# Values and gates of the recurrence as one 2x2x2 block product in seven multiplications

## The chip, the core and the metric

The kernel runs on one core of a Trainium2 chip. The core has a matrix engine (TensorE, PE in the profile, with its weight loads as PEld), a vector engine (VectorE, DVE), an activation engine (ScalarE, ACT), a general engine (GpSimd, POOL), a queue that issues transfers (SyncE, SP) and 16 DMA engines. Every engine works through its own list of instructions in order and waits on semaphores for the others. The metric is the device time of one execution in microseconds; less is better.

## The reference, cut to what matters

```python
hn = rmsnorm(h, norm_mix_g[l])                 # 512 tokens x 1024
proj = hn @ w_in[l]
fq, fk, fv, ff, gq, gf, gi, gg = jnp.split(proj, split_idx, axis=-1)
...
rec = hgrn2_chunkwise(gq, gf, gi, lbs[l])      # gi: the values, 512 columns
rec = rmsnorm(rec, hgrn_norm_g[l]) * jax.nn.silu(gg...)   # gg: the gates, 512 columns
```

One layer follows: forgetting attention (fq, fk, fv, ff), the gated recurrence (gq, gf, gi, gg), an output projection, cross attention on 256 memory tokens, and an MLP with 4096 hidden columns. The change is in how gi and gg are computed: together they are the product of hn (512 x 1024) with 1024 columns of w_in.

## The kernel before

**Products.** Activations and weights are split into a high part (one conversion on ACT) and a low part (the difference, on DVE), and every product is three matmuls: high by high, high by low, low by high. Weights come as panels of 1 MB in two halves (a and b) of 512 KB. SP loads a half into one of two raw buffers (`wrN` in the profile, N the panel's number), ACT writes the high part `whN`, DVE the low part `wlN`; high and low parts have four buffers each, so two panels. A raw buffer can be loaded again when both parts are written, and a high or low buffer can be written again when PE is through with the half that lay there.

**Order.** PE's instructions run as the code writes them; ACT, DVE, POOL and SP have orders that a scheduler lays down when the kernel is built. `next_panel` (L216) loads up to two panels ahead of use. The panels are: 0 and 1 the forget logits gf, 2 and 3 the queries gq, 4 the first 256 value columns and the 8 forget columns of the attention (`proj_if`), 5 and 6 the gates (`proj_wide`), 7 and 8 the other 256 value columns together with 256 columns of fv (`proj_iv`), then 9 onwards the pairs of attention heads.

**Fill.** The recurrence needs an attention matrix inside each chunk, made in seven levels (m = 1, 2, 4 .. 64; L800 on PE, L806, L825 and L826 on DVE and POOL). Between two levels PE has nothing of its own to do, so `Fill` runs pieces of the projections there: `fill.run(us)` by a budget, `fill.until(name)` until a named projection is done. After the levels come the transposes `pa` of the attention matrix, the transposes `pk` of the keys, and the recurrence's steps (`po`, `pst`), which need the values `iv` and the gates `gg`.

**Block products in seven.** The MLP already multiplies 2 x 2 blocks in seven products (`SEVEN`), with sums of weight blocks made in DRAM: SP copies a block into a DRAM buffer (`copies`, so many behind each load by the table `COPIES`), and POOL adds another block to it with an accumulating transfer (`presum`, paced by PE's work through `PACE`).

**The residual.** `x_park` (L507) copies the transposed x of each column block out of PSUM and POOL writes it to DRAM (`xTd`), where the output projection fetches it later.

Of the kernel before, what the change touches and what calls it, by code (L numbers as in the profile page):

```python
# [16 lines left out]
P = 128  # L17
S = 512
# [20 lines left out]
NEG = -3.0e38  # L39
SEVEN = (1, 2, 3, 4, 5, 6, 7)  # L40
RAWS, HB, LOADS = 5, 4, 8
COPIES = {7: 2, 16: 1, 17: 0, 21: 1}
PACE = (183.0, 4.7), (306.0, 11.5)


@with_exitstack
def emit(
# [81 lines left out]
    def f(a):  # L129
        return a.bitcast(F32)  # L130
# [277 lines left out]
    gp.affine_select(out=tri[:, 0, :], in_=tri[:, 0, :], compare_op=ALU.is_ge, fill=0.0, base=0, pattern=[[1, P]], channel_multiplier=-1)  # L408


    hn_hi, hn_lo = act_tile("hn_hi"), act_tile("hn_lo")
    xTd = drp.tile([4, P, 2, S], F32, name="xTd")

# [73 lines left out]
    park = {}  # L487

    ms0 = sm(NT, "ms0")
    gv = cp.tile([P, 33], F32, name="gv")  # L490
# [14 lines left out]
        ve.scalar_tensor_tensor(hn_lo[:, c, :], xps[c], g_mix[:, c : c + 1], f(hn_hi[:, c, :]), op0=ALU.mult, op1=ALU.subtract)  # L505

    def x_park(c):  # L507
        part, new_ = c // 2, c // 2 not in park
        if new_:
            park[part] = s4([2, S], f"xT{part}")  # L510
        dst = park[part][:, c % 2, :]
        if c % 2 == 0:
            ac.activation(dst, xps[c], AF.Copy)
        else:
            ve.tensor_copy(dst, xps[c])
        if not new_:
            gp.dma_start(xTd[part], park[part])

    def x_sq(tb):
        junk = s4([D], f"x0j{tb}")  # L520
# [8 lines left out]
    with tc.manual_schedule(engines={mybir.EngineType.Activation, mybir.EngineType.DVE}):  # L529
# [121 lines left out]
    g_x, g_mem, g_ff, g_h = gv[:, 0:8], gv[:, 8:16], gv[:, 16:24], gv[:, 24:25]  # L651
    gate(3)
    forget(3)
    for hp in range(2):
        wt = next_panel()
        for j in range(2):
# [17 lines left out]
    def proj_wide(dsts, func, name):  # L674

        pss = [mm(f"{name}{tb}") for tb in range(NT - 1)] + [pvt(f"{name}3")]
        n = S // len(dsts)

        def done(tb, ps):
            for i, dst in enumerate(dsts):  # L680
                ac.activation(dst(tb), ps[:, i * n : (i + 1) * n], func, scale=r0[:, tb : tb + 1])

        yield from gemm_wide(pss, hn_hi, hn_lo, done)
# [4 lines left out]
    z = sm(32, "z")  # L688
    z3 = z.rearrange("p (t h) -> p t h", h=FH)

    def proj_if():
        wt = next_panel()
        for tb in range(NT):
            ps = mm(f"gi0{tb}", (WT + FH,))
            yield from gemm_tm(ps, wt, hn_hi, hn_lo, tb)
            ac.activation(iv[tb // 2][:, tb % 2, 0:WT], ps[:, 0:WT], AF.Identity, scale=r0[:, tb : tb + 1])
# [7 lines left out]
    fill.add(proj_if(), "ff")  # L704
    fill.add(new(gg, "gg"))
    fill.add(proj_wide([lambda tb: gg[tb // 2][:, tb % 2, :]], AF.Silu, "gg"), "gg")
# [6 lines left out]
    def proj_iv():  # L713
        yield from proj_wide([lambda tb: iv[tb // 2][:, tb % 2, WT:S], new_fv()], AF.Identity, "gi")

    fill.add(proj_iv(), "iv")

# [181 lines left out]
    load_mem(0)  # L899


    mx_hi, mx_lo = act_tile("mx_hi"), act_tile("mx_lo")
    St = None
    pending = None

# [1013 lines left out]
```

## Time and profile before

| | |
|---|---|
| median of 3 runs | 752.15 us (751.25 to 752.2) |
| the profiled execution | 751.99 us |
| its span, first to last instruction | 750.3 us |
| PE busy | 742.9 us of the span |
| DVE, ACT, POOL busy | 546.5, 444.7, 202.1 us |
| granted TensorE clock | 0.998 |

The profiled execution is 1.69 us longer than its span; that is what lies around the instructions. The first 62 us of the span are the norm, the forget logits and the queries, the levels run to 111 us, the recurrence to 158 us, then attention, output projection, cross attention and from 429 us the MLP.

### The profile page before, as it was taken

How to read it: one execution, taken by the hardware profiler on the slowest of the kernel's cores; microseconds unless marked ns; L12 is line 12 of the kernel's file. 1: busy time of each engine (PE TensorE's matmuls, PEld its weight loads, DVE VectorE, ACT ScalarE, POOL GpSimd, SP SyncE). 2: the span in 40 equal slices, each digit the busy share in tenths (PEclk: the TensorE clock that was granted, in tenths of full speed). 3: DMA queues.
4: the chain of work that ended last, by engine and by line, in shares of the span. 5: the costliest groups of instructions: out<-in, count | busy, mean ns of one | idle time of the engine just before them, and what ended most of it. 6: DMA issues, size and time to landing. Idle time of an engine off the chain costs nothing.

```text
span 750.3 us, 12293 instructions
## 1 busy us (share of the span) xinstructions
PE 742.9 (99%) x4581; PEld 649.6 (87%) x4581; DVE 546.5 (73%) x869; ACT 444.7 (59%) x749; POOL 202.1 (27%) x280
## 2 busy tenths in 40 slices
PE   9999999999999999999999999999999999999996
PEld 6889888888888888888888899898989899999985
DVE  5647873667878856645556898978787887878796
ACT  5655555556666742344434589666566757574864
POOL 7207531233433237621111212111111111100034
PEclk9999999999999999999999999999999999999999
DMA  8641987578957889985579799898989898978452
GB/s 250 200 116 58 298 262 228 172 231 269 289 187 224 265 225 210 193 165 122 121 165 197 114 250 238 237 226 247 230 218 235 220 247 214 240 198 232 133 113 113
DMA packets 109678, 152.92 MB, mean 204 GB/s; under 512 B 6145, under 2 KB 76074, under 8 KB 109618
## 3 DMA queue, kind: packets, MB, share of 16 engines
q1 hardware_dynamic: 85458, 112.52, 46.3%
q0 software_dynamic: 24000, 39.35, 30.1%
q8 instruction: 36, 0.59, 0.3%
q14 instruction: 24, 0.20, 0.1%
q10 hardware_dynamic: 160, 0.27, 0.1%
HBM read 147.91 MB, written 51.40 MB: 266 GB/s over the span
## 4 chain that ended last, share of the span: by engine, by line
PE 96%; DVE 1%; issue 1%; ACT 0%; POOL 0%; POOLq 0%; DVEq 0%
PE uU L1494 4%; PE uU L1496 4%; PE uU L1495 4%; PE U L1652 3%; PE U L1653 3%; PE U L1654 3%; PE uY L1495 2%; PE uY L1494 2%; PE uY L1496 2%; PE xk L1008 2%; PE xq L253 2%; PE wo L253 2%; PE xq L254 2%; PE xq L255 2%; PE xw L255 2%; PE xw L254 2%
## 5 line engine op out<-in xcount | busy, mean ns | idle before, releaser
L183 DVE TENSOR_TENSOR wlu<-wru,whu 128x1024 fp32r<-128x1024 f32 x53 | 64.2, 1225 | 28.0 <-ACT whu L179 27.9
L179 ACT ACTIVATE whu<-wru 128x1024 fp32r<-128x1024 f32 x53 | 55.9, 1058 | 43.7 <-PE U L1654 16.8
L183 DVE TENSOR_TENSOR wld<-wrd,whd 128x1024 fp32r<-128x1024 f32 x56 | 68.3, 1222 | 13.5 <-ACT whd L179 13.2
L179 ACT ACTIVATE whd<-wrd 128x1024 fp32r<-128x1024 f32 x56 | 59.0, 1053 | 12.6 <-PE uU L1495 5.2
L1652 PE MATMUL U<-whd,hb 128*128 128x512 f32 x120 | 46.8, 390 | 0.0
L1653 PE MATMUL U<-wld,hb 128*128 128x512 f32 x120 | 46.8, 390 | 0.0
L1654 PE MATMUL U<-whd,hb 128*128 128x512 f32 x120 | 46.7, 389 | 0.0
L1029 POOL TENSOR_SCALAR bi<-nF,Ft 128x128 f32<-128x128 f32 (+3 forms) x32 | 20.6, 652 | 59.8 <-PE pt L1065 38.8
L1494 PE MATMUL uU<-xs_hi,whu 128*128 128x256 f32 x128 | 36.3, 284 | 0.0
L1496 PE MATMUL uU<-xs_hi,wlu 128*128 128x256 f32 x128 | 36.2, 283 | 0.0
L1495 PE MATMUL uY<-xs_lo,whu 128*128 128x256 f32 x128 | 36.2, 283 | 0.0
L1494 PE MATMUL uY<-xs_hi,whu 128*128 128x256 f32 x128 | 36.2, 283 | 0.0
L1496 PE MATMUL uU<-x_hi,wlu 128*128 128x256 f32 x128 | 36.2, 283 | 0.0
L1496 PE MATMUL uY<-xs_hi,wlu 128*128 128x256 f32 x128 | 36.2, 283 | 0.0
L1495 PE MATMUL uU<-xs_lo,whu 128*128 128x256 f32 x128 | 36.2, 283 | 0.0
L1495 PE MATMUL uU<-x_lo,whu 128*128 128x256 f32 x128 | 36.2, 283 | 0.0
L1494 PE MATMUL uU<-x_hi,whu 128*128 128x256 f32 x128 | 36.2, 283 | 0.0
L444 POOL DMA_DIRECT2D wsd<-in_w_dram x16 | 17.9, 1116 | 63.6 <-PE xw L255 12.8
L1390 POOL DMA_DIRECT2D wrd<-in_w_dram x8 | 9.8, 1221 | 86.2 <-DVE wld L183 85.0
L444 POOL DMA_DIRECT2D wsu<-in_w_dram x14 | 17.1, 1218 | 48.9 <-PE xw L255 15.6
L1654 PEld LDWEIGHTS U<-whd,hb 128*128 128x128 f32 x120 | 22.5, 188 | 4.7
L1652 PEld LDWEIGHTS U<-whd,hb 128*128 128x128 f32 x120 | 22.6, 188 | 4.5
(944 smaller groups left out, 2605.2 us busy)
## 6 DMA issues: line engine op xcount, KB each, us to landing
wru<-in_w_dram SPq DMA_DIRECT2D x25, 512.0 KB, 7.9
wsd<-in_w_dram SPq DMA_DIRECT2D x24, 512.0 KB, 7.3
wrd<-in_w_dram SPq DMA_DIRECT2D x24, 512.0 KB, 4.3
wrd<-wsd SPq DMA_DIRECT2D x24, 512.0 KB, 4.9
wsu<-in_w_dram SPq DMA_DIRECT2D x21, 512.0 KB, 5.6
wru<-wsu SPq DMA_DIRECT2D x21, 512.0 KB, 6.1
wsd<-in_w_dram POOLq DMA_DIRECT2D x16, 512.0 KB, 7.8
wsu<-in_w_dram POOLq DMA_DIRECT2D x14, 512.0 KB, 6.9
```

Of the source, the lines that this page charges most:

```text
L179: at = ac.activation(hi, raw, AF.Copy)
L183: at_lo = ve.tensor_tensor(lo, raw, f(hi), ALU.subtract)
L253: te.matmul(ps, wh, hi, start=n_ == 0 and not begun, stop=False)
L254: te.matmul(ps, wh, lo, start=False, stop=False)
L255: at = te.matmul(ps, wl, hi, start=False, stop=k == order[-1])
L444: yield gp.dma_start(wsum[kind, g, name], src, accum_op=ALU.add, **more)
L1494: te.matmul(ps[:, i, :], whi[:, k, ws], xh[:, k, :], start=begin, stop=False, skip_group_check=True)
L1495: te.matmul(ps[:, i, :], whi[:, k, ws], xl[:, k, :], start=False, stop=False, skip_group_check=True)
L1496: at = te.matmul(ps[:, i, :], wlo[:, k, ws], xh[:, k, :], start=False, stop=k == UK - 1, skip_group_check=True)
L1652: te.matmul(ps, hi, whi[:, k, :], start=begin, stop=False, skip_group_check=True)
L1653: te.matmul(ps, hi, wlo[:, k, :], start=False, stop=False, skip_group_check=True)
L1654: at = te.matmul(ps, lo, whi[:, k, :], start=False, stop=k == 1, skip_group_check=True)
```

## The change

The 512 value columns and the 512 gate columns become one product of 2 x 2 blocks: the tokens in two halves of 256, the inner dimension in two halves of 512, the columns as values and gates. Seven products of (256 tokens, 512 inner, 512 columns) replace eight. Four of them take a sum of weight blocks, four a sum of token blocks.

- `token_sums` and `token_parts` form the token sums before the second pair of gq panels: ACT scales the parked x in place by the norm's gain, DVE forms four combinations, ACT and DVE split them into high and low parts in the buffers that later hold the mixer's output (`mx_hi`, `mx_lo`).
- The weight sums lie in DRAM: eight copies of 512 KB on SP behind the loads of panels 2 and 3 (`COPIES` at 2), and eight accumulating transfers of 512 KB on POOL (`gate_sums_w`), where the third pair needs the first landed and the fourth the third.
- `seven` runs the products in the order 1, 5, 6, 3, 7, 2, 4 in two sets of accumulators, U and W, which are read out in between and then added to further.
- The forget columns move from the first value panel to the first fv panel (`proj_ff`), which is loaded in its place.
- There are 1 + 7 panels where there were 1 + 4; `COPIES` is shifted by three panels and `PACE` by 5 us of PE's work.
- x is parked in one buffer of the activation pool (`park`) and no longer in four of the pool `s4`.

```diff
-COPIES = {7: 2, 16: 1, 17: 0, 21: 1}
-PACE = (183.0, 4.7), (306.0, 11.5)
+COPIES = {2: 2, 4: 0, 10: 2, 19: 1, 20: 0, 24: 1}
+PACE = (178.0, 4.7), (301.0, 11.5)
...
-    for n0 in (2056, 2312, 1544, 1800, 2568):
+    for n0 in (2056, 2312, 1544, 1800, 1024):
         specs.append(panel(w_in, n0))
-    specs += wide(w_in, 3080)
-    specs += wide(w_in, 2824, 1024)
+    GSUMS = {"5": ("00", "01"), "7": ("01", "11"), "6": ("11", "5"), "4": ("10", "6")}
+    GORDER = ("1", "5", "6", "3", "7", "2", "4")
...
+    for name in GORDER:
+        specs.append([(slice(0, S), gsum[name] if name in GSUMS else block0({"1": "00", "2": "10", "3": "11"}[name]))])
...
+    for name, (a, _) in GSUMS.items():
+        for ks in (slice(0, 2), slice(2, 4)):
+            copies.append(lambda name=name, a=a, ks=ks: nc.sync.dma_start(gsum[name][:, ks, :], block0(a)[:, ks, :]))
+
+    def gate_sums_w():
+        for name, (_, b) in GSUMS.items():
+            for ks in (slice(0, 2), slice(2, 4)):
+                src, more = (gsum[b][:, ks, :], {"max_dma_last_dim": 2048}) if b in GSUMS else (block0(b)[:, ks, :], {})
+                tc.keep_in_program_order(gp.dma_start(gsum[name][:, ks, :], src, accum_op=ALU.add, **more))
...
+    def token_sums():
+        for c in range(KC):
+            ac.activation(park[:, c, :], park[:, c, :], AF.Identity, scale=g_mix[:, c : c + 1])
+        A1a, A2a, A1b, A2b = (park[:, ks, h] for ks in (slice(0, 4), slice(4, 8)) for h in (h1, h2))
...
+        ve.tensor_tensor(hdif["5"], A2b, A2a, ALU.subtract)
+        ve.tensor_tensor(hdif["6"], hdif["5"], A1a, ALU.add)
+        ve.tensor_tensor(hdif["3"], hdif["6"], A1b, ALU.subtract)
+        ve.tensor_tensor(hdif["7"], A1a, A2a, ALU.subtract)
+
+    def token_parts():
...
+            ac.activation(hi, hdif[name], AF.Copy, scale=sign)
+            ve.scalar_tensor_tensor(lo, hdif[name], sign, f(hi), op0=ALU.mult, op1=ALU.subtract)
...
+        def done(name, t, ps):
+            if name == "1":
+                ac.activation(tok(iv, t), ps, AF.Identity, scale=r0[:, t : t + 1])
+            elif name == "2":
+                ve.scalar_tensor_tensor(tok(iv, t), ps, r0[:, t : t + 1], tok(iv, t), op0=ALU.mult, op1=ALU.add)
+            elif name == "4":
+                ac.activation(tok(iv, 2 + t), ps, AF.Identity, scale=r0[:, 2 + t : 3 + t])
+            elif name in "56":
+                ac.activation(tok(gg, t + (2 if name == "5" else 0)), ps, AF.Copy)
+            else:
...
+                ve.tensor_tensor(g_, ps, g_, ALU.add)
+                ac.activation(g_, g_, AF.Silu, scale=nr0[:, tb : tb + 1])
...
+            for u in range(2):
+                for t, ps in enumerate(pss):
+                    ts_ = slice(t * P, (t + 1) * P)
+                    for kk in range(2):
+                        k = 2 * u + kk
+                        hi, lo, begin, end = xh[:, k, ts_], xl[:, k, ts_], name in "125" and k == 0, k == 3
+                        te.matmul(ps, hi, whi[u][:, kk, :], start=begin, stop=False, skip_group_check=True)
+                        te.matmul(ps, hi, wlo[u][:, kk, :], start=False, stop=False, skip_group_check=True)
+                        at = te.matmul(ps, lo, whi[u][:, kk, :], start=False, stop=end, skip_group_check=True)
+                        yield presum.tick(3 * S / 2400, at)
...
-    fill.add(proj_iv(), "iv")
+    fill.add(proj_ff(), "ff")
+    fill.add(new(gg, "gg"))
+    fill.add(seven(GORDER[:5]), "gg")
+    fill.add(seven(GORDER[5:]), "iv")
```

How the orders change shows at three places. The first is POOL between the write of the residual and the first multiplications of the recurrence. Before (`xTd` is the residual in DRAM, `mov` and `sta` hold keys and queries, `F` the forget gates):

```order
L605 DMA fb<-in_fox_f_bias_dram 128x8 [waits Pool_49]
L517 DMA xTd<-xT_408 128x1024 [waits DVE_49,Activation_49]
L517 DMA xTd<-xT_468 128x1024 [waits DVE_49]
L734 TENSOR_TENSOR mov_459<-mov_459,F_458 128x512 [waits PE_49,Activation_49]
L734 TENSOR_TENSOR sta_460<-sta_460,F_458 128x512 [waits PE_49,Activation_49]
```

Now (`wsg_105`, `106`, `107` and `108` are the sums for products 5, 7, 6 and 4):

```order
L534 DMA xTd<-park 128x1024 [waits DVE_49]
L497 DMA wsg_105<-in_w_in_dram 128x2x512 [waits DMAHW2_49]
L497 DMA wsg_105<-in_w_in_dram 128x2x512 [waits DMAHW3_49]
L497 DMA wsg_106<-in_w_in_dram 128x2x512 [waits DMAHW5_49]
L497 DMA wsg_106<-in_w_in_dram 128x2x512 [waits DMAHW6_49,DMASW0_49]
L497 DMA wsg_107<-wsg_105 128x2x512 [waits DMAHW0_49,DMASW5_49,DMASW1_49]
L497 DMA wsg_107<-wsg_105 128x2x512 [waits DMAHW1_49,DMASW6_49,DMASW2_49]
L497 DMA wsg_108<-wsg_107 128x2x512 [waits DMAHW3_49,DMASW3_49,DMASW1_49]
L497 DMA wsg_108<-wsg_107 128x2x512 [waits DMAHW4_49,DMASW4_49,DMASW2_49]
L826 TENSOR_TENSOR mov_465<-mov_465,F_464 128x512 [waits PE_49,Activation_49]
```

Eight transfers, five of which wait for earlier ones of POOL's own, stand in front of the multiplications.

The second is DVE around level m = 32. Before (`Ac` is the attention matrix, `lv` a level's product):

```order
L825 TENSOR_TENSOR sta_463<-sta_463,F_461 128x8x32 [waits DVE_49]
L183 TENSOR_TENSOR wl8b<-wr8b,wh8b 128x1024 [waits DMAHW1_49,DMAHW2_49,PE_49,Activation_49]
L758 COPY Ft<-pF 128x32 [waits PE_49]
L806 COPY_PREDICATED Ac_656<-mku,lv_1205 128x4x32 [waits DVE_49,PE_49]
L825 TENSOR_TENSOR mov_459<-mov_459,F_458 128x8x32 [waits DVE_49]
L806 COPY_PREDICATED Ac_725<-mku,lv_1214 128x4x32 [waits DVE_49,PE_49]
L825 TENSOR_TENSOR mov_462<-mov_462,F_461 128x8x32 [waits DVE_49]
```

Now, in the same stretch:

```order
L917 TENSOR_TENSOR sta_469<-sta_469,F_467 128x8x32 [waits DVE_49]
L850 COPY Ft<-pF 128x32 [waits PE_49]
L898 COPY_PREDICATED Ac_701<-mku,lv_1268 128x4x32 [waits DVE_49,PE_49]
L917 TENSOR_TENSOR mov_465<-mov_465,F_464 128x8x32 [waits DVE_49]
L191 TENSOR_TENSOR wl10b<-wr10b,wh10b 128x1024 [waits DMAHW6_49,Activation_49]
L898 COPY_PREDICATED Ac_771<-mku,lv_1277 128x4x32 [waits DVE_49,PE_49]
L917 TENSOR_TENSOR mov_468<-mov_468,F_467 128x8x32 [waits DVE_49]
L781 TENSOR_TENSOR gg_917<-gU_918,gg_917 128x512 [waits PE_49]
L781 TENSOR_TENSOR gg_917<-gU_919,gg_917 128x512 [waits PE_49]
L191 TENSOR_TENSOR wl11a<-wr11a,wh11a 128x1024 [waits DMAHW1_49,Activation_49]
```

A low part stands between the two heads' parts of a level, and two additions to the gates and the next low part behind them.

The third is the end of the levels, on ACT. Before (`A<-pa` puts the transposed attention matrix back):

```order
L179 ACTIVATE wh9b<-wr9b 128x1024 [waits DMAHW2_49,DMAHW1_49,PE_49]
L179 ACTIVATE wh10a<-wr10a 128x1024 [waits DMAHW6_49,DMAHW5_49,PE_49]
L879 ACTIVATE A_1288<-pa_1365 128x512 [waits PE_49,DVE_49,Activation_49,Pool_49]
L879 ACTIVATE A_1300<-pa_1374 128x512 [waits PE_49,DVE_49,Activation_49,Pool_49]
L681 ACTIVATE iv_653<-gi_1167,r_434 128x256 [waits PE_49]
```

Now:

```order
L187 ACTIVATE wh11b<-wr11b 128x1024 [waits DMAHW4_49,PE_49]
L187 ACTIVATE wh12a<-wr12a 128x1024 [waits DMAHW7_49,DMAHW0_49,PE_49]
L775 ACTIVATE iv_699<-gU_918,r_440 128x512 [waits PE_49]
L775 ACTIVATE iv_699<-gU_919,r_440 128x512 [waits PE_49]
L187 ACTIVATE wh12b<-wr12b 128x1024 [waits DMAHW4_49,DMAHW3_49]
L971 ACTIVATE A_1371<-pa_1451 128x512 [waits DVE_49,PE_49,Pool_49]
L971 ACTIVATE A_1383<-pa_1483 128x512 [waits PE_49,DVE_49,Activation_49,Pool_49]
```

Panel 12, the first pair of attention heads (panel 9 before), is used directly behind the levels, and the high part of its second half stands ahead of the attention matrix on ACT.

More of the change, by code (lines that the diff above doesn't have):

```diff
@@ L486, in emit @@
     presum.jobs.extend(j for _, j in sets)
-    park = {}
     ms0 = sm(NT, "ms0")
@@ L507, in x_park @@
     def x_park(c):
[L508 to L511, printed above, removed]
+        part, dst = c // 2, park[:, c, :]
         if c % 2 == 0:
@@ L515, in x_park @@
             ve.tensor_copy(dst, xps[c])
-        if not new_:
-            gp.dma_start(xTd[part], park[part])
+        parked.add(c)
+        if c ^ 1 in parked:
+            gp.dma_start(xTd[part], park[:, 2 * part : 2 * part + 2, :])
     def x_sq(tb):
@@ L653, in emit @@
     forget(3)
+    mx_hi = act_tile("mx_hi")
+    nr0 = sm(NT, "nr0")
+    ve.tensor_scalar(nr0, r0, -1.0, None, op0=ALU.mult)
+    hsum, hdif = {}, {}
+    h1, h2 = slice(0, WT), slice(WT, S)
+    def token_sums():
+        for c in range(KC):
+            ac.activation(park[:, c, :], park[:, c, :], AF.Identity, scale=g_mix[:, c : c + 1])
+        A1a, A2a, A1b, A2b = (park[:, ks, h] for ks in (slice(0, 4), slice(4, 8)) for h in (h1, h2))
+        for name in "5637":
+            hdif[name] = k4([4, WT], f"hd{name}")
+        ve.tensor_tensor(hdif["5"], A2b, A2a, ALU.subtract)
[3 more added lines that the diff above has]
+    def token_parts():
+        hs = [t.rearrange("p k (h n) -> p (k h) n", h=2) for t in (mx_hi, mx_lo)]
+        for i, name in enumerate("5637"):
+            hi, lo = hsum[name] = [t[:, 4 * i : 4 * i + 4, :] for t in hs]
+            sign = -1.0 if name == "6" else 1.0
+            ac.activation(hi, hdif[name], AF.Copy, scale=sign)
+            ve.scalar_tensor_tensor(lo, hdif[name], sign, f(hi), op0=ALU.mult, op1=ALU.subtract)
+        for name, ks, h in (("1", slice(0, 4), h1), ("2", slice(4, 8), h1), ("4", slice(4, 8), h2)):
+            hsum[name] = hn_hi[:, ks, h], hn_lo[:, ks, h]
     for hp in range(2):
         wt = next_panel()
+        if hp == 0:
+            assert len(copied) == 0 and len(stream) > 3
+            gate_sums_w()
+        if hp == 1:
+            token_sums()
+            mx_lo = act_tile("mx_lo")
+            token_parts()
         for j in range(2):
@@ L689, in emit, with proj_ff @@
     z3 = z.rearrange("p (t h) -> p t h", h=FH)
-    def proj_if():
+    def proj_ff():
         wt = next_panel()
+        dst = new_fv()
         for tb in range(NT):
@@ L702, in new @@
         yield
-    fill.add(proj_if(), "ff")
-    fill.add(new(gg, "gg"))
-    fill.add(proj_wide([lambda tb: gg[tb // 2][:, tb % 2, :]], AF.Silu, "gg"), "gg")
     def new_fv():
@@ L711, in new_fv, with seven, tok @@
         return lambda tb, n0=0: t[:, tb, :]
-    def proj_iv():
-        yield from proj_wide([lambda tb: iv[tb // 2][:, tb % 2, WT:S], new_fv()], AF.Identity, "gi")
-    fill.add(proj_iv(), "iv")
+    U, W = [], []
+    def seven(names):
+        def tok(ts, tb):
+            return ts[tb // 2][:, tb % 2, :]
+        def done(name, t, ps):
[8 more added lines that the diff above has]
+            else:
+                tb = t + (2 if name == "7" else 0)
+                g_ = tok(gg, tb)
+                ve.tensor_tensor(g_, ps, g_, ALU.add)
+                ac.activation(g_, g_, AF.Silu, scale=nr0[:, tb : tb + 1])
+        for name in names:
+            if name == "1":
+                U.extend(mm(f"gU{t}") for t in range(2))
+            elif name == "5":
+                W.extend((mm("gW0"), pvt("gW1")))
+            pss = U if name in "1674" else W
+            whi, wlo = next_panel()
+            xh, xl = hsum[name]
+            for u in range(2):
[8 more added lines that the diff above has]
+                        yield presum.tick(3 * S / 2400, at)
+                    if u == 1:
+                        done(name, t, ps)
+    fill.add(proj_ff(), "ff")
+    fill.add(new(gg, "gg"))
+    fill.add(seven(GORDER[:5]), "gg")
+    fill.add(seven(GORDER[5:]), "iv")
     Ac = []
@@ L899, in emit @@
     load_mem(0)
-    mx_hi, mx_lo = act_tile("mx_hi"), act_tile("mx_lo")
     St = None
```

8 lines of the change are left out of this document (7 added, 1 removed).

## The prediction

> **What bounds the kernel now.** I read the page first (busy time, slices, chain), then stretches of time.
>
> ```profile
> span 750.3 us, 12293 instructions
> PE 742.9 (99%) x4581; PEld 649.6 (87%) x4581; DVE 546.5 (73%) x869; ACT 444.7 (59%) x749; POOL 202.1 (27%) x280
> PE   9999999999999999999999999999999999999996
> PE 96%; DVE 1%; issue 1%; ACT 0%; POOL 0%; POOLq 0%; DVEq 0%
> ```
>
> PE is busy in every slice but the last, and the chain that ended last is PE for 96% of the span. So a matmul that goes away is worth its whole duration, and any moment in which PE waits is a loss that nothing pays back. Two clean rows in the queries give the price of a matmul:
>
> ```profile
> 44.63 0.39 PE L253 MATMUL gq<-hn_hi,wh3a 128*128 128x512 f32 x1
> ...
> 50.07 0.39 PE L253 MATMUL gq<-hn_hi,wh3a 128*128 128x512 f32 x1
> ```
>
> Between these starts lie 24 matmuls of 512 columns: 5.44 us, 0.227 us each (the 0.39 us shown overlaps with the next).
>
> **What is taken away.** Gates, values and the fv columns beside them took 192 such matmuls (panels 5 to 8), the seven products take 168; the 96 matmuls of 264 columns stay, now for fv and the forget columns. The gain is 24 x 0.227 = 5.44 us, and by the orders of PE exactly 24 rows are gone. Up to the first transpose of the attention matrix (`pa`) PE's order keeps the same number of matmuls between the same levels; the 24 are missing behind it, between `pa` and the recurrence's steps (9) and in the third step (15). So the gain comes late, and what feeds PE ahead of it must deliver in the same time as before 7 panels where it delivered 3 1/2.
>
> **Early: weight sums in DRAM.** Eight copies and eight accumulating transfers of 0.524 MB are new between 22 and about 60 us.
>
> ```profile
> 20.00:30.00 10.00, 10.00 (x49) 8.10 (x48) 8.24 (x17) 6.33 (x11) 3.98 (x6) 1.00 0.64 197
> 30.00:40.00 10.00, 10.00 (x46) 8.29 (x45) 5.49 (x6) 7.67 (x13) 0.00 (x0) 1.00 0.51 158
> 40.00:50.00 10.00, 10.00 (x46) 8.29 (x45) 4.43 (x5) 6.02 (x7) 0.00 (x0) 1.00 0.62 162
> 50.00:60.00 10.00, 10.00 (x85) 8.68 (x84) 5.25 (x6) 3.31 (x5) 3.51 (x2) 1.00 0.39 108
> 60.00:72.00 12.00, 12.00 (x140) 11.41 (x140) 8.79 (x19) 5.52 (x15) 7.98 (x10) 1.00 0.14 45
> ...
> q1 hardware_dynamic: 85458, 112.52, 46.3%
> q0 software_dynamic: 24000, 39.35, 30.1%
> DMA to landing us min/median/max: 5.4/7.1/11.4
> ...
> 29.34 0.53 POOL L517 DMA_DIRECT2D xTd<-xT  x1 [2.15 <-DVE xT L515]
> ...
> 56.45 1.28 POOL L734 TENSOR_TENSOR mov<-mov,F 128x512 f32<-128x512 f32 x1 [26.59 <-PE dg L730]
> 57.69 2.28 POOL L734 TENSOR_TENSOR sta<-sta,F 128x512 f32<-128x512 f32 x1
> ...
> 62.59 1.48 POOL L734 TENSOR_TENSOR sta<-sta,F 128x512 f32<-128x512 f32 x1
> ```
>
> (In the stretches the last two numbers are the DMA engines' share and GB/s; the landing row is that of the MLP's accumulating transfers.) q1 moves 112.52 MB in 46.3% of the span, 0.324 MB/us, so a copy takes 1.6 us of all 16 engines; q0 39.35 MB in 30.1%, 0.174 MB/us, so an accumulation takes 3.0 us. Who waits: POOL must issue all eight accumulations before the multiplications that stood idle 26.59 us until 56.45, and its last pair waits for the third to land, which waits for the first. From 30 us, with landings of 7.1 us and 1.1 us of issue each, the first lands at 38, the third at 46, and POOL is free at about 48. Its four multiplications take some 6 us and were done at 64.07 only since the second pair waited for PE; free by 58.3 it loses nothing. That is the low bound, no loss. The high bound: up to the third pair's first landing eight copies and five accumulations need 13 + 15 = 28 us of engines; the shares leave 18.4 us free up to 60 and 10.3 up to 72, so if the loads always went first POOL would be free at 73, 15 us late. The two queues take turns, so I put it at 59 to 60. What is late then is the first level, for which `mov` and `sta` must be ready, and PE behind it. The same traffic sits ahead of panel 3's second half:
>
> ```profile
> 32.48 0.37 SPq L205 DMA_DIRECT2D wr3b<-in_w_in_dram  x1
> ...
> 47.35 0.39 PE L253 MATMUL gq<-hn_hi,wh3b 128*128 128x512 f32 x1
> ```
>
> Now wr3a and two copies (4.9 us of engines) stand before it, with the rest of the copies before them (1.6). At full rate it lands near 41, with half the rate near 48; PE wants the split 47.4. So none to 3 us late; a PE delay here also gives POOL that time. I take 1.5 us for both, bounds 0 and 15.
>
> **Early: token sums.** DVE gets four sums and four low parts, ACT eight scalings and four high parts:
>
> ```profile
> L183 DVE TENSOR_TENSOR wlu<-wru,whu 128x1024 fp32r<-128x1024 f32 x53 | 64.2, 1225 | 28.0 <-ACT whu L179 27.9
> L179 ACT ACTIVATE whu<-wru 128x1024 fp32r<-128x1024 f32 x53 | 55.9, 1058 | 43.7 <-PE U L1654 16.8
> L632 DVE TENSOR_TENSOR sg<-gf,rbc 128x512 f32<-128x512 f32 x4 | 2.7, 687 | 0.9 <-PE gf L255 0.9
> L681 ACT ACTIVATE gg<-gg,r 128x512 f32<-128x512 f32 x4 | 2.6, 684 | 0.4 <-PE gg L283 0.4
> ```
>
> By these rows 8 x 1.23 = 9.8 us on DVE and at most 8 x 0.68 + 4 x 1.06 = 9.7 on ACT, in the stretches 20 to 60, where DVE is busy 23.4 and ACT 23.3 of 40 us. The in-place scaling waits until the residual's write has landed (about 33 for the last), with the sigmoids queued behind it. PE's 96 query matmuls cover this; the low parts of panel 4, due at 56.7, come at about 54. Nothing, and if the cover failed the lag of those low parts would be the price. The residual itself still leaves with four transfers.
>
> **The levels.** Seven panels of 24 matmuls are used from 71 us to `pa`:
>
> ```profile
> 72.54 1.08 PE lv L800 x32
> 79.99 1.08 PE lv L800 x32
> 86.73 1.08 PE lv L800 x32
> ...
> 109.17 1.79 PE lv L800 x16
> 118.45 0.44 PE pa L878 x4
> ...
> 72.00:80.00 8.00, 8.00 (x64) 6.19 (x64) 6.91 (x14) 6.76 (x13) 4.96 (x4) 1.00 0.56 171
> 80.00:87.00 7.00, 7.00 (x66) 5.69 (x68) 5.42 (x15) 3.13 (x8) 3.81 (x4) 1.00 1.03 343
> 87.00:94.00 7.00, 7.00 (x56) 5.67 (x51) 4.90 (x12) 3.21 (x7) 3.29 (x4) 1.00 0.85 273
> 94.00:101.00 7.00, 7.00 (x60) 5.87 (x60) 5.13 (x12) 6.54 (x11) 3.22 (x6) 1.00 0.93 300
> 101.00:109.00 8.00, 8.00 (x66) 6.62 (x66) 4.97 (x13) 4.43 (x7) 2.00 (x4) 1.00 0.72 216
> 109.00:118.00 9.00, 9.00 (x50) 7.78 (x49) 5.32 (x8) 1.06 (x1) 2.88 (x6) 1.00 0.82 257
> ...
> wr2a<-in_w_in_dram SPq DMA_DIRECT2D x1, 512.0 KB, 3.7
> ```
>
> A panel per 6.8 us. A raw buffer goes round in 3.7 (issue to landing) + 1.06 + 1.23 = 6.0 us, and there are two, one per half: it fits with 0.8 us to spare for waits in the queues of ACT and DVE. DVE's load: the six stretches add up to 32.7 us of 46. New are 4 low parts (8 fell there, now 12), 4.9 us; four additions to the gates and two to the values at 0.69, 4.1 us: 41.7 of 46, 91%. ACT goes from 25.1 to about 25.1 + 4 x 1.06 + 6 x 0.68 = 33.4. Low bound no loss. High bound: DVE's idle 13.3 us are waits for ACT, POOL and PE; if all of them stayed, 41.7 + 13.3 = 55.0 would be 9 us more than 46. As the halves come out ready 0.5 to 4 us ahead of PE when I lay these durations along the new orders, I take 0.7.
>
> **The end of the levels.** From panel 10 on each half brings two MLP copies, 1.57 MB, which at 0.343 MB/us (the stretch from 80) takes 4.6 us. Panel 10's first half is issued at about 94.5, and 12b, five halves later, starts at 117.4 and lands at about 121 (1.5 us of transfer, 2.1 of latency out of the 3.7). ACT splits it until 122.1 and only then copies the attention matrix back:
>
> ```profile
> 125.29 0.89 PE po L934 x8
> ...
> L879 ACT ACTIVATE A<-pa x2: 578/588/598, 119.5 to 120.2; 128x512 f32<-128x512 f32 x2
> ```
>
> Two copies end at 123.3; `po`, 9 matmuls earlier than before, would want them at 125.29 - 2.04 = 123.25 and the second half's low part at 122.8 against 123.3. I take 0.8; bounds 0 (loads meet no queue) and 3 (one more pair of copies in front, with its split).
>
> Sum: 750.3 - 5.44 + 1.5 + 0.7 + 0.8 = 747.9 span; with the 1.69 us around it 749.5, and as the profiled run (751.99) stands 0.16 under the median, 749.7 in its terms. The MLP's sums keep their place in PE's work (`PACE` moves by about the 24 matmuls), so I count nothing there.
>
> **A rule on the port.** The rows show DVE and POOL in each other's way:
>
> ```profile
> 56.93 1.88 DVE L183 TENSOR_TENSOR wl5b<-wr5b,wh5b 128x1024 fp32r<-128x1024 f32 x1
> ```
>
> 1.88 against 1.23 us for a low part, while POOL's `sta` above took 2.28 against 1.48. The Trainium skill, "SBUF — State Buffer", section "Who interferes with whom", says that a DVE instruction with two SBUF inputs and a GpSimd instruction that reads SBUF block each other for the whole instruction; these rows agree. What it would cost here is rival 2.
>
> **Rivals.** (1) *No stall at all*: each transfer lands as the low bounds have it; 750.3 - 5.44 + 1.85 = 746.7. For it speaks that PE has no wait in the levels now; against it 28 us of engines in 18. (2) *Port*: each of the 12 low parts in the levels meets a POOL multiplication and takes 0.65 more, 7.8 us on DVE, 49.5 of 46: 3.5 us in place of 0.7, in all 752.5, no change. Against it: only wl5b and one other low part are stretched now. (3) *Accumulations hold POOL*: the third pair lands late in the shared engines, POOL is free at 67, the first level is 8.7 us late; with 0.7 and 0.8 the time is 750.3 - 5.44 + 10.2 + 1.85 = 756.9, slower. It decides from a POOL free at 62.2 (58.3 + 5.44 - 1.5). For it: the 18.4 us; against it: the landings of 7.1 us among equally heavy traffic in the MLP. (4) *DVE keeps its waits* in the levels: 9 us as above with 0.8 and 1.5 early, 750.3 - 5.44 + 11.3 + 1.85 = 758.0.
>
> **How the numbers follow.** 0.2% (1.5 us) is about what a measurement of this kernel tells from no change. Forecast 0.45 (747.5 to 750.6 of its own); (1) 0.10; (2) 0.10; (3) 0.22; (4) 0.13. Faster 0.55, same 0.10, slower 0.35. The range goes from 746.5, just under the full gain, to 757.5, which leaves out more than half of (4) and the worst of (3), and little else.
>
> **What would show it.** PE should run without a gap to 44 us, and 24 fewer matmuls should be counted. `mov` on POOL starting by 58 shows the accumulations harmless, at 62 or later rival 3. PE waiting at `gq` for `wl3b`: the load behind the copies. Levels 7.3 us apart on average as now show the feeding to hold; more, with DVE above 90%, rival 4, or 2 where the low parts are above 1.6 us. A gap at `po` behind `A<-pa`: the last term. The forecast is wrong if PE's idle time between 30 and 130 us is above 5 us, or below 0.5.

## The result, and the profile after

| | before | after |
|---|---|---|
| median | 752.08 us (751.25 to 752.2, 4 runs) | 770.43 us (767.67 to 771.08, 4 runs) |
| span of the profiled execution | 750.3 us | 768.8 us |
| first level (`lv`, m = 1) on PE | 65.42 us | 84.31 us |
| last level (m = 64) | 109.0 us | 128.67 us |
| first `po` (the recurrence's steps) | 125.13 us | 146.36 us |
| first `ps` (attention scores) | 158.03 us | 175.88 us |

The change made the kernel slower: 1.0239 times the time before, interval 1.0214 to 1.0265. From the page of the changed kernel, busy time and slices (span / 40 = 19.2 us each), granted clock, chain of waits:

```profile
span 768.8 us, 12322 instructions
PE 744.8 (97%) x4557; PEld 647.9 (84%) x4557; DVE 567.6 (74%) x890; ACT 460.3 (60%) x767; POOL 212.3 (28%) x288
PE   9948999899999999999999999999999999999996
PEclk9987999999999999999999999999999999999999
PE 79%; DMA 8%; DVE 6%; ACT 3%; issue 2%; POOL 0%; SPq 0%; POOLq 0%; DVEq 0%; ACTq 0%
```

PE has the 24 matmuls less (4557 against 4581), yet is busy 1.9 us longer, with a hole in its third slice and a lowered clock in the third and fourth. Before, DMA stood at nothing in the chain; now it has 8% of the span. The table of starts says where: PE is 18.9 us late at the first level, 19.7 at the last, 21.2 at `po`, and 17.9 at `ps`. Nearly all is lost before the first level. PE's waits, in all, times, longest:

```profile
PE gq L261 <- ACT wh3b L187: 9.2, 1, 9.2
PE gi L275 <- DVE wl4a L191: 1.4, 1, 1.4
...
PE pk L1008 <- ACT A L971: 1.1, 1, 1.1
PE gU L799 <- DVE wl11b L191: 1.1, 1, 1.1
PE gq L261 <- ACT wh3a L187: 0.8, 1, 0.8
PE gi L275 <- DVE wl4b L191: 0.7, 1, 0.7
PE pt L1156 <- DVE dn L1143: 0.6, 1, 0.6
PE pq L263 <- DVE wl12a L191: 0.6, 1, 0.6
PE gq L263 <- DVE wl3a L191: 0.5, 1, 0.5
PE gi L274 <- ACT wh4a L187: 0.3, 1, 0.3
```

The six waits for panels 3 and 4 make 12.9 us, and behind each stands a load. First the queue of SP, then ACT, which turns raw halves into high parts (start, duration, in brackets its wait):

```profile
30.60 0.37 SPq L213 DMA_DIRECT2D wr3a<-in_w_in_dram  x1
31.02 1.44 SPq L491 DMA_DIRECT2D wsg<-in_w_in_dram  x2
32.57 0.55 SPq L213 DMA_DIRECT2D wr3b<-in_w_in_dram  x1
33.16 10.72 SPq L491 DMA_DIRECT2D wsg<-in_w_in_dram  x2
46.08 7.30 SPq L213 DMA_DIRECT2D wr4a<-in_w_in_dram  x2
59.13 3.35 SPq L213 DMA_DIRECT2D wr4b<-in_w_in_dram  x2
```

```profile
43.74 1.06 ACT L187 ACTIVATE wh3a<-wr3a 128x1024 fp32r<-128x1024 f32 x1 [2.94 <-DMA wr3a<-in_w_in_dram]
...
56.79 1.06 ACT L187 ACTIVATE wh3b<-wr3b 128x1024 fp32r<-128x1024 f32 x1 [9.02 <-DMA wr3b<-in_w_in_dram]
...
68.83 1.08 ACT L187 ACTIVATE wh4a<-wr4a 128x1056 fp32r<-128x1056 f32 x1 [4.72 <-DMA wr4a<-in_w_in_dram]
73.01 1.08 ACT L187 ACTIVATE wh4b<-wr4b 128x1056 fp32r<-128x1056 f32 x1 [3.10 <-DMA wr4b<-in_w_in_dram]
```

wr3a takes 13 us from issue to use, wr3b 24, wr4a 23. They hang together: wr4a uses the raw buffer of wr3a, so it can't be issued before `wl3a` has ended at 46.06; wr4b, issued at 59.13, stands in the same way behind `wl3b`, which ended at 59.11. POOL, the engine the prediction watched, was not what PE waited for. Its last accumulation was issued at 64.57, and `mov` then stood 3.65 us waiting for PE:

```profile
64.57 1.14 POOL L497 DMA_DIRECT2D wsg<-wsg  x1 [2.79 <-DMA wsg<-wsg]
69.35 1.26 POOL L826 TENSOR_TENSOR mov<-mov,F 128x512 f32<-128x512 f32 x1 [3.65 <-PE dg L822]
```

12.9 us are not 18.9. The rest shows in stretches (length; PE busy and instructions; PEld, DVE, ACT, POOL; then clock, DMA share, GB/s). In the first and the last of these three PE works at about half its clock:

```profile
57.90:62.94 5.04, 5.00 (x12) 3.54 (x13) 3.98 (x4) 5.03 (x6) 1.14 (x1) 0.58 1.07 220
62.94:68.40 5.46, 5.46 (x25) 4.32 (x23) 2.55 (x3) 1.16 (x2) 1.14 (x1) 1.00 1.10 204
72.00:79.40 7.40, 6.64 (x31) 5.88 (x30) 4.35 (x6) 3.39 (x5) 0.86 (x1) 0.54 0.51 143
```

The 12 matmuls behind the long wait took 5.04 us and not 12 x 0.227 = 2.72; the 30 of 264 columns from 72 us came 0.22 us apart and not 0.12. That is 2.3 and about 3 us.

### The profile page after: what moved, and what is told of

It reads as the page before. It is cut to its first block, busy times and chain, and to the rows that moved or that the text cites. A ratio compares the mean times of both kernels' runs of the same rounds, so it can differ in the third digit from the quotient of the medians.

```text
span 768.8 us, 12322 instructions
## 1 busy us (share of the span) xinstructions
PE 744.8 (97%) x4557; PEld 647.9 (84%) x4557; DVE 567.6 (74%) x890; ACT 460.3 (60%) x767; POOL 212.3 (28%) x288
## 4 chain that ended last, share of the span: by engine, by line
PE 79%; DMA 8%; DVE 6%; ACT 3%; issue 2%; POOL 0%; SPq 0%; POOLq 0%; DVEq 0%; ACTq 0%
PE uU L1585 4%; PE uU L1587 4%; PE uU L1586 4%; PE U L1743 3%; PE U L1744 3%; PE U L1745 3%; DMA wr3b<-in_w_in_dram 3%; PE uY L1586 2%; PE uY L1585 2%; PE uY L1587 2%; PE xk L1099 2%; PE xq L261 2%; PE wo L261 2%; PE xq L262 2%; PE xq L263 2%
## 5 line engine op out<-in xcount | busy, mean ns | idle before, releaser
L1120 POOL TENSOR_SCALAR bi<-nF,Ft 128x128 f32<-128x128 f32 (+3 forms) x32 | 21.2, 671 | 59.6 <-PE pt L1156 42.7
```

The source lines that it names most:

```text
L1120: gp.tensor_scalar(bi[:, 0:n], fF[h][:, 0:n], -1.0, Ft[:, tb, h : h + 1], op0=ALU.mult, op1=ALU.add)
```

## The experiments

Unless a range is given, each is one run beside one of the kernel before (751.29 to 751.84 us there), and differences below 1.5 us are not read. Edits are against the changed kernel.

### Which part costs the time

**Without the sums.** Edit: no copies, no accumulations, the sum panels load plain blocks.

```diff
-COPIES = {2: 2, 4: 0, 10: 2, 19: 1, 20: 0, 24: 1}
+COPIES = {10: 2, 19: 1, 20: 0, 24: 1}
...
-            gate_sums_w()
```

> The weight sums are left out: no copies, no accumulating transfers, and the four panels that held sums load a plain block each, so the values and gates are not those of the reference; the seven products, token sums and splits stay. Theory (the transfers of the weight sums keep the panel loads away): PE's waits of 14 us before the levels and the lowered clock are gone, 748 to 750 us. Rival (the seven products themselves, with more low parts on DVE and a panel per 6.8 us, are too much for the feeding): 755 us or more, with PE waits in the levels.

Measured: 752.04 us. No wait for panel 3 or 4 is left, so the sums cost all of the 18 us. But the 5.44 us of the 24 matmuls did not appear either; the last group of runs is about that.

**Copies alone.** Edit: `gate_sums_w()` left out, the copies stay, panels load the unfinished buffers.

> The accumulating transfers are left out, so the sum panels hold one block only; the eight copies stay where they are. If the loads of panels 3 and 4 are late because they stand behind the copies in SP's queue: panel 3b still lands 10 us or more after its issue, and the time stays above 758 us. If the accumulating transfers take the DMA engines from them: 3b lands in 8 us and the time is 748 to 753 us.

Measured: 752.95 us. The copies, six of them in front of wr3b in SP's queue and two behind it, cost 0.9 us, which is less than can be read; the place behind them is not the cause. The accumulations are worth 770.4 - 753.0 = 17.5 us.

**Copies from ACT's queue.** Edit: `ac.dma_start` for `nc.sync.dma_start` in the copies.

> The eight copies are issued from ACT's queue in place of SP's, at the same places; everything else as in the changed kernel. If it is the place behind the copies in one queue: panel 3b lands in some 8 us, and the time falls below 760 us. If it is the amount of traffic in the engines whatever the queue: it stays within 4 us of 770.

Measured: 768.65 us, with the waits moved (`gi`<-`wl4b` 3.3, `gq`<-`wh3a` 2.8). The copies now had a queue of their own (q10 in the profile, 4.46 MB against 0.27 in the changed kernel), and the loads were left alone in SP's. They still got little: from 38 to 44 us they moved 0.39 MB in 389 packets, beside 379 of POOL's. Whose queue carries the copies matters little.

**The kernel before with the traffic added.** Edit to the kernel before: the eight copies and eight accumulations, with nothing reading them.

> The kernel before with the change's eight copies and eight accumulating transfers added at the same places, their result unused; products as before. Theory: the traffic alone costs what the change lost before the levels, 15 to 22 us, so 767 to 774 us, with PE waiting for wh3b and wl4. Rival (the new token sums on ACT and DVE or the products carry part of it): below 762 us.

Measured: 774.3 us, 22.6 above the kernel before and 0.3 above the range that was expected, with waits at the same places (`wh3b` 6.3, `wh4a` 3.0). So the traffic does it by itself; token sums, order of products and read-outs aren't needed.

### Why the loads starve

The DMA engines' share from 20 to 90 us without sums, with copies, and in the changed kernel:

```profile
20.00:90.00 70.00, 70.00 (x515) 59.37 (x515) 58.02 (x91) 50.82 (x82) 24.93 (x28) 1.00 0.46 131
```

```profile
20.00:90.00 70.00, 69.45 (x511) 58.66 (x512) 55.84 (x90) 49.18 (x79) 24.47 (x28) 1.00 0.59 186
```

```profile
20.00:90.00 70.00, 56.93 (x351) 47.08 (x351) 39.48 (x57) 35.95 (x55) 24.15 (x22) 0.88 0.85 215
```

0.13 of 70 us is 9.1 for eight copies, 1.1 each; 0.26 is 18.2 for the accumulations, and four half panels less were loaded by then (some 5.4 us at the 0.39 MB/us of the copies' best slices), so about 3.0 each. Together some 33 us, where 38 were free. Over the whole stretch it would have fitted; it did not fit into the time in which panels 3 and 4 had to land (the engines' share from 33 to 57 us is 1.08; a share above 1 means that packet times overlap). From 33 to 44 us the two queues (packets, MB, share of all 16 engines; q1 is SP's, q0 POOL's), in the changed kernel and with copies alone:

```profile
q0 software_dynamic: 773, 1.67, 78.0%
q1 hardware_dynamic: 723, 0.89, 29.0%
```

```profile
q1 hardware_dynamic: 2232, 3.31, 88.0%
q0 software_dynamic: 160, 0.55, 14.2%
```

Beside the accumulations q1 moved 0.89 MB in 11 us, without them 3.31. Its packets are about as many as q0's, but a packet of q0 takes 0.78 x 11 x 16 / 773 = 0.18 us of an engine, one of q1 0.07. The counts agree best while both queues have work: 433 of q0 and 435 of q1 from 38 to 44 us. From 50 to 57 us, where POOL's accumulations wait for earlier ones, they are 285 and 964, so the loads lost their share before that.

**Half of the sums.** Edit: `GSUMS` holds only sums 5 and 7, so four copies and four accumulations.

> The change with two of the four weight sums (5 and 7: four copies behind panel 2, four accumulations); panels 6 and 4 of the product load a plain block, so gates and values are not the reference's. If the loss goes with the number of accumulations: half of 17 us, 760 to 762. If only what exceeds the free time of the DMA engines costs (4 copies and 4 accumulations need 6.4 + 12.0 = 18.4 us of all 16 engines, and 18.4 were free up to 60 us): 752 to 755. If it is the chain of pairs that wait for each other (third behind the first, fourth behind the third), which is gone here: 752.

Measured: 757.7 us, between two of the answers: 5.7 above the run without sums, a third of the loss for half of the transfers. A loss that grows faster than the traffic fits engines that fill up, but neither figure was right. The chain of pairs is gone here and a loss of 5.7 us stays, so the chain isn't needed for it.

**Plain transfers in place of accumulations.** Edit: POOL sends the same blocks to other buffers, without adding.

```diff
-tc.keep_in_program_order(gp.dma_start(gsum[name][:, ks, :], src, accum_op=ALU.add, **more))
+tc.keep_in_program_order(gp.dma_start(gplain[name][:, ks, :], src, **more))
```

> The change with its eight accumulating transfers turned into plain ones of the same blocks into other DRAM buffers, in the same places of POOL's list and with the same waits (the sum panels get plain blocks, so gates and values are not the reference's). Theory (an accumulation reads twice and writes once, and takes about twice a copy's time of the DMA engines, 3.0 against 1.6 us; the loss comes from the part beyond the free time): with 8 x 1.6 us less of the engines' time in the crowded stretch most of the 17 us go, 753 to 760. Rival (it is POOL's queue as such, which takes turns with SP's whatever it carries, or the chain of pairs): 765 or more.

Measured: 762.64 us, again between both: 9.7 above copies alone, 7.8 below the change. Up to 44 us POOL's plain transfers push the loads aside as much:

```profile
q0 software_dynamic: 746, 2.72, 78.7%
q1 hardware_dynamic: 702, 0.85, 26.5%
```

They only end sooner, for they carry 2.72 MB in the time in which accumulations carry 1.67.

**Accumulations in smaller pieces.** Edit: each in two by columns, rows of 1 KB and not 2 KB.

```diff
+for ns in (slice(0, WT), slice(WT, S)):
+    src = (gsum[b] if b in GSUMS else block0(b))[:, ks, ns]
+    tc.keep_in_program_order(gp.dma_start(gsum[name][:, ks, ns], src, accum_op=ALU.add))
```

> The change with each accumulation made in two by columns (256 columns, rows of 1 KB in place of 2 KB; 16 of them, the same bytes). From 33 to 44 us the two queues moved about as many packets (773 of POOL's, 723 of SP's), but POOL's took 78% of the engines' time and SP's 29%: 0.18 us a packet against 0.07. If the queues take turns packet by packet, smaller pieces on POOL's side give the loads a larger share in that stretch (q1 40% or more, at least 1.3 MB in place of 0.89), wr3b is split by 50 to 53 rather than at 56.8, and the time falls to 762 to 767 although the accumulations last longer. If the share goes by bytes or by time, or POOL's queue goes first, q1 stays at 25 to 33% and the time at 769 or more.

Measured: 773.07 us. From 33 to 44 us:

```profile
q0 software_dynamic: 1038, 1.35, 65.2%
q1 hardware_dynamic: 1031, 1.49, 47.5%
```

The mechanism holds: 1038 packets against 1031, and the loads now move 1.49 MB. `wh3b` starts at 53.60 and not 56.79 (50 to 53 had been expected). From 44 to 57 us:

```profile
q0 software_dynamic: 1371, 1.32, 64.0%
q1 hardware_dynamic: 1369, 2.02, 51.9%
```

But the time did not fall, as I had said it would: the accumulations last longer, `wh4b` starts at 73.10 as before, and PE waits 3.1 us for `wl4a`. Turns by packets decide who is late first; when the last load is in seems to follow from the sum of the work, which no run here sets apart. The Trainium skill, "DMA: Bandwidth & Descriptors", section "Queues, rings and completion order", says that each engine goes round its queues a packet at a time; these counts agree with equal turns. Whether a packet of the profile is what that page calls one, no run here shows.

### Can the sums be placed better?

**Late sums.** Edit: one copy behind each half of panels 3 to 6, sum 5 where it was, the others later.

```diff
-COPIES = {2: 2, 4: 0, 10: 2, 19: 1, 20: 0, 24: 1}
+COPIES = {3: 1, 7: 0, 10: 2, 19: 1, 20: 0, 24: 1}
...
+        if hp == 1:
+            gate_sums_w("6")
         fill.run(2 * F1)
...
+        if li in (0, 2):
+            gate_sums_w("74"[li // 2])
```

> The change with the same eight copies and eight accumulations, but spread out: one copy behind each half of panels 3 to 6, the accumulations of sum 5 where they were, those of sum 6 behind the sta multiplications, of sum 7 behind the first level, of sum 4 behind the third. Theory (what costs is that the accumulations are crowded into the stretch in which panels 3 and 4 have to land): the 17 us between the change and the same kernel without accumulations shrink to 0 to 4, in all 750 to 757, and PE does not wait for wh3b. Rival (an accumulation costs PE about 2 us wherever it lies, since it always holds up some load): 765 or more, with the waits moved to the panels of the levels.

Measured: 763.38 us, between both. PE no longer waits for panels 3 to 6; ACT waits 5.2 us for the load of sum 6, and through ACT's list `mov` (3.1) and the values (2.3) are late.

**Sums in between.** Edit: as above, sum 6 directly behind sum 5, sum 7 and 4 a step earlier, nF read earlier (see below).

> The copies spread out as before (one behind each half of panels 3 to 6), the accumulations a step earlier than in the run with late sums: sum 6 directly behind sum 5, sum 7 behind the sta multiplications, sum 4 behind the first level; and nF is read one recurrence step earlier. Theory (the spread run lost its time because wh7a, wh9a and wh11a waited for sums that landed late, with ACT standing at them; the DMA engines had room at 85 to 95 us): the waits lv<-mov 3.1 and gU<-iv 2.3 and pt<-dn 2.4 go, 750 to 756. Rival (the accumulations need more of the DMA engines than is free anywhere ahead of 110 us): the waits move to panels 4 and 5, 760 or more.

Measured: 765.05 us, but my edit was wrong: sum 6 was added ahead of its copy in the program, so the copies waited for the accumulation and overwrote it. The run says nothing on the question.

**Sums in order.** Edit: sum 6 behind the second pair of gq panels, where its copy has been issued; sum 4 behind the second level.

> What the run with the sums between meant to be: one copy behind each half of panels 3 to 6, and every accumulation behind its copy in the program (there sum 6 was added before its copy was made, so that the copies waited for it and the sum was lost): sum 5 at the first pair of gq panels, sum 6 at the second, sum 7 behind the sta multiplications, sum 4 behind the second level; nF read a step earlier. If only the late landing of sums 6, 7 and 4 cost the late run its time (waits lv<-mov 3.1, gU<-iv 2.3, pt<-dn 2.4): 752 to 756. If the engines' time is short wherever the sums lie: 758 or more, with the waits at other panels.

Measured: 762.36 us, on the side of the second answer. That the engines' time is short wherever the sums lie isn't shown by it: their share was 0.67, 0.70 and 0.61 in the three stretches of 10 us from 80 us on. The longest wait is now `dg`<-`Ac`, 3.8 us; DVE shows what it stood behind:

```profile
61.42 1.22 DVE L191 TENSOR_TENSOR wl5a<-wr5a,wh5a 128x1024 fp32r<-128x1024 f32 x1 [5.99 <-ACT wh5a L187]
62.56 0.68 DVE L715 TENSOR_TENSOR sta<-gq,rbc 128x512 f32<-128x512 f32 x1
63.16 0.74 DVE L829 TENSOR_TENSOR Ac<-dg,id 128x256 f32<-128x256 f32 x2
```

wr5a, issued at 52.03, was not in until 60.33. A late load no longer hits its own matmul but whatever stands behind its split.

**Half of the sums in order.** Edit: sums 5 and 7 alone, placed so, nF earlier.

> Two of the four sums (5 and 7, spread out: copies behind the halves of panels 3 and 4, sum 5 added at the first gq pair, sum 7 behind the sta multiplications), nF a step earlier; panels 6 and 4 of the product load plain blocks, so gates and values are not the reference's. With half the traffic in the free places the theory (crowding, not the number) says what the kernel without sums and nF early gave, 749 to 750.5; if each accumulation has its price, 752 or more.

Measured: 752.2 us, on the side of "each has its price", though only just: 3.2 above the same without sums (748.99, below), or 3.7 if each is taken against the kernel before in its own job. PE has no wait before 108 us. The price now lies at the end of the levels (`wl11b` 1.1, `wh11b` 0.7, `S` 0.5, and a clock of 0.94 and 0.89 from 110 to 130), where the MLP's copies run beside the loads of panels 10 and 11. Why it does so is not shown: the engines are as full there in the run without sums and with nF early (1.05, 1.03 and 1.07 from 100 to 130 us, against 1.00, 1.02 and 1.05 here). Placed well, four accumulations fall from 5.7 (by the run with half the sums) to 3.2 us; not to nothing.

### What the lowered clock is

**PE kept busy.** Edit: idle matmuls ahead of the waits, 36 before panel 3's second half and 18 before the first `gi`.

```diff
+    def keep_busy(n):
+        idle_ = pvt(f"idle{n}")
+        for _ in range(n):
+            te.matmul(idle_, hn_hi[:, 0, 0:P], hn_hi[:, 0, :], start=True, stop=True)
...
+                if h == 2 and n_ == 3:
+                    keep_busy(36)
...
+        keep_busy(18)
```

> The change with 36 idle matmuls of 512 columns ahead of the first one that needs panel 3's second half (8.2 us in a wait of 9.2) and 18 ahead of the first gi matmul (4.1 us in the waits there); their results are not used. If the rest of the loss behind the waits (some 5 us: matmuls of 512 columns at 0.43 us apart from 58 to 62, those of 264 at 0.22 from 72 to 79) comes of the lower granted clock after PE stood idle, the clock stays at 1.0 through both stretches, and the second dg comes some 3 us earlier than at 79.4: 766 to 768. If the matmuls were slow for another reason (weights, reads of memory that the transfers fill), they stay slow: 770 or more.

Measured: 774.61 us. The same stretches as above, first the 12 matmuls behind the wait, then the first `gi`, then those behind the next wait:

```profile
58.05:60.77 2.72, 2.72 (x14) 2.25 (x12) 1.65 (x3) 2.72 (x4) 0.84 (x1) 1.00 1.06 236
...
71.50:75.20 3.70, 3.70 (x32) 3.64 (x30) 1.07 (x2) 0.63 (x1) 0.00 (x0) 1.00 0.84 273
80.00:84.00 4.00, 3.83 (x30) 3.74 (x31) 3.46 (x8) 1.96 (x6) 2.11 (x2) 0.57 0.51 175
```

Just as many matmuls, the same loads under way, and 2.72 us for 5.04: it was the clock, and the clock came from PE standing still. But the first level came at 86.13 and not 84.31, so the time I had forecast for this was wrong. PE was early for the next link: it waited 3.3 us for `Ac` behind `wl5a`, idle again, and the clock fell there (0.57 from 80 us). Loads set the pace, and a busy PE only waits elsewhere. The Trainium skill, "TensorE: Matmul & The Clock Gate", section "What's actually happening", has the clock at half behind an idle window of some 3.4 us; 0.58 behind the gap of 9.2 us fits it. The gap of 3.3 us, with 0.57 behind it, is a little shorter than that. The clock also fell behind a single wait of 1.7 us (0.61, in the run without sums, below), and at 72 us in the changed kernel, behind waits of 0.3 and 1.4 us with short matmuls between them. Neither follows from that rule, and both stay open.

### Where the gain of 5.44 us went

Without sums PE is 3.25 us ahead at `ps` (154.78 against 158.03) and level with the kernel before at 166.5. In between POOL's list and PE's wait in that run:

```profile
148.85 0.37 POOL L1117 TENSOR_SCALAR bi<-nF,Ft 128x128 f32<-128x128 f32 x1
150.72 0.38 POOL L1117 TENSOR_SCALAR bi<-nF,Ft 128x128 f32<-128x128 f32 x1 [1.50 <-DMA nF<-Fd]
...
153.40 0.56 POOL L385 TENSOR_TENSOR m1r<-m1re,mhalf 128x1 f32<-128x1 f32 x1
```

```profile
PE pt L1153 <- DVE dn L1140: 1.7, 1, 1.7
```

POOL waits for nF (the cumulative forget logits), m1r stands behind it, DVE's next instruction waits for m1r, and `dn` (the softmax's divisor, ahead of PE's transposes `pt`) follows that by 7.44 us in both traces (155.53 to 162.97 before, 153.99 to 161.43 here). Then PE has stood still, and runs at 0.61 from 162 to 166.

**nF read earlier.** Edit to the kernel without sums: the read one recurrence step earlier, `MT, NF = 3, 1` for `3, 2`.

> The kernel without sums (it leaves out the weight sums, so its values and gates are not the reference's) with the two reads of the cumulative forget logits (nF) issued one recurrence step earlier. Theory (behind the levels POOL waits for nF to land, m1r stands behind it in POOL's list, and the first softmax behind m1r in DVE's): POOL waits no longer at bi, pt comes without a wait of 1.7 us, the clock stays at 1.0 in the stretch from 162 to 166, and 2 to 3.5 us come back: 748.5 to 750. Rival (the chain of softmax steps on DVE itself is too long for the shortened work of PE): pt waits as before, 752.

Measured: 748.99 us, 2.85 under the kernel before in the same job, within the forecast. POOL's wait, the wait at `pt` and the lowered clock are gone. Left are 1.3 us of waits at the end of the levels.

**MLP copies two panels earlier.** Edit to the kernel without sums: `COPIES = {8: 2, 17: 1, 18: 0, 22: 1}`.

> The kernel without sums (it leaves out the weight sums, so its values and gates are not the reference's) with the MLP's copies starting two panels earlier, behind panel 8 rather than 10. Theory (the copies, begun some 17 us later than before the change, fill the DMA engines from 100 to 154 us, where the kernel before had them idle at 138 to 146; nF, wl11b and wl12a are late because of it): those waits go and the time is 748.5 to 750. Rival (the same transfers only jam two panels earlier, in the levels): new waits for panels 8 to 10, 752 or more.

Measured: 757.82 us, the rival's side: new waits for panel 10 (3.4 us in four) and panel 12 (1.1). The wait at `pt` is gone, as foreseen, but the copies meet the panels of the levels.

**The change, and the kernel before, with nF earlier.** The same one number in each.

> The change as it is, with nF read one recurrence step earlier. In the kernel without sums this gave 3.0 us; here pt waits for dn 0.6 us and the clock is whole there, so by the theory 0.6 to 1 us come back, 769 to 770; were the delay in the softmax worth the same here, 767.

> The kernel before with nF read one recurrence step earlier. It has no wait at pt (softmax ready at 163.56, PE there at 163.60), so by the theory nothing changes: 751.5 to 752.5. If the earlier read is worth something by itself (not as a cure of what the change brought): 750 or less.

Measured: 768.17 us, 2.3 under the median of the change, with the wait at `pt` gone; but single runs of the change spread over 3.4 us, so this is not read further. The kernel before: 751.5 us against 751.29, no difference, since nothing waited there.

No version with the right sums came out ahead of the kernel before; the best was 762.36 us.

## Why the prediction was wrong

- **"What is taken away" was right.** 24 matmuls fewer. Without the sums PE was 3.25 us ahead at `ps` (1.6 us of the rest went into waits at the end of the levels), and 2.85 us were left at the end once nF was early.
- **"Early: weight sums in DRAM" failed**, taken as 1.5 us with 15 as its highest, measured 18.9 at the first level. Its prices held: a copy 1.1 us (1.6 taken), an accumulation about 3.0, as taken. The step that failed is "The two queues take turns", read there as half the rate each: "with half the rate near 48", and so "none to 3 us late". They take turns by packets, and beside packets of 0.18 us those of the loads, 0.07 us, got 29% and not half: 0.89 MB from 33 to 44 us, where half of the prediction's 0.324 MB/us would have been 1.78. wr3b was used from 56.79 and not 48.
- **The high bound looked at the wrong one.** It supposed "if the loads always went first POOL would be free at 73", and priced PE through `mov` and `sta`. POOL was free at 65.7, later than the 59 to 60 and the 62.2 from which rival 3 decides, and PE still came later, held by loads. So rival 3 was right about the shared engines and wrong about who is held. No bound asked what happens if the loads go last, nor that wr4a waits for wr3a's raw buffer, which hands the delay on.
- **Nothing was set down for the clock.** 12.9 us of waits brought some 5.3 more.
- **"Early: token sums" at nothing**: no wait of PE points to them; not tried apart from the rest.
- **"The levels", 0.7**: PE lost 0.8 from the first to the last (7.39 us apart, 7.26 before); rivals 2 and 4 did not come.
- **"The end of the levels", 0.8, bounds 0 to 3**: the right place and too small. `A` behind `wh12b` came as written (1.1), with `wl11b` 1.1 and `wl12a` 0.6: 2.8 us of waits. From the last level to `po` PE took 17.69 us and not 16.13, with 2.04 us of matmuls less: 3.6 us lost where 0.8 was taken. The miss adds up from that: 17.4 us too little in the early term, 0.1 in the levels, 2.8 here, and 0.6 at `pt`, which was not in the sum; together 20.9, against 770.4 - 749.7 = 20.7.
- **Unforeseen behind the levels**: shortening PE's work ahead of `pt` brings out POOL's read of nF. The prediction counted the gain as kept from `po` on.
- "Wrong if PE's idle time between 30 and 130 us is above 5 us" is what came: its waits there add up to 12.9.

## What to carry to other kernels

Transfers that fit into the free time of the DMA engines are not free: ask which load stands beside them, and compare the time that one packet of each queue takes, since the queue with the longer packets takes the larger share. A load that is late once hands its delay on through the buffer that it frees, and a wait of PE can cost more than its length, as the clock may fall behind it. And where PE's work is shortened, look for the next chain on POOL and DVE that had just enough cover.

## What the runs showed of the hardware

- Two queues with work for the same engines moved equal numbers of packets: 1371 and 1369 in 13 us, 1038 and 1031 in 11 (accumulations in small pieces), 433 and 435 in 6 (the changed kernel).
- By the engines' shares from 20 to 90 us, an accumulating transfer of 512 KB took an estimated 3.0 us of all 16 engines, a copy in DRAM 1.1. With the accumulations under way, the 512 KB load wr3a landed 13.1 us after its issue, with copies alone 6.5.
- SP was held by its own issues: two copies issued at 33.16 took 10.72 us, where 1.99 were enough without accumulations.
- Behind an idle stretch of 9.2 us matmuls of 512 columns came 0.43 us apart for about 4 us, then 0.23 again; with PE kept busy ahead of the same matmuls they never slowed.
